# A hybrid mLSTM and sparse-attention block: moving the gate rows, a compression's gelu, a bank and a piece of a query projection

## The chip, the cores and the metric

The kernel runs on one core of a Trainium2 chip, in fp32. Its engines are TensorE (PE; its weight loads are listed as PEld), VectorE (DVE), ScalarE (ACT), GpSimd (POOL) and SyncE (SP, which here only issues transfers). Each works off its own queue of instructions in order. The metric is the device time of one execution in microseconds (us), the median of several.

## The reference, cut to what matters

One transformer block on 512 tokens of width 1024: a projection of the normed input feeds an mLSTM with 4 heads and an attention with 8 heads in 2 groups; then come the output projection, a feed-forward layer with a convolution, and a gated embedding. Only the beginning of it is touched by the change:

```
z = rms_norm(x, ln1_g) @ w_in
mq, mk, mv, mo, mi, mf, aq, akc, avc, aks, avs, akw, avw, ag = split(z)

def mlstm(q, k, v, i_pre, f_pre):              # in chunks; per head:
    b = cumsum(log_sigmoid(f_pre))             # forget gates, summed along the tokens
    a = bL - b + i_pre
    m = maximum(b + m_before, max(D))          # D = b_t - b_s + i_s for s <= t
    ...

def compress(t, pe, w1, w2):                   # for keys (Kc) and for values (Vc)
    blk = t[:, :, cidx] + pe                   # 31 blocks of 32 tokens
    return gelu(flat @ w1) @ w2

s_c = qblk @ Kc - slope * dist                 # scores: compressed, selected and window
```

## The kernel before, in words

**Products in three parts.** A weight `w` is split into a rounded high part (`hi`, a copy on ACT, L151) and the rest (`lo`, a subtraction on DVE, L152), and so is the input (`xh`, `xl`). A product is `hi*xh + hi*xl` for all its blocks, then `lo*xh`. PE therefore asks for a weight's high split when a job starts and for its low split after two thirds of the job. Two buffers hold high splits and two hold low ones, so a split waits until PE has left the job two before it.

**The stream.** `Stream` holds jobs (weight, function that writes its matmuls) in the order k1 q00 m0 w00 q01 w01 m1 w10 m2 w11 m3, then q10 q11, mo0 to mo3, mq0 to mq7. q, k, mo and mq are 8 blocks of 512 columns into a bank of tag G; m0 to m3 (`mv` in the trace) sum the mLSTM's values over two blocks each into four banks (the pair of tag Sa and two of tag T); wXY is half Y of the first compression product of kv = X (0 keys, 1 values; `cw` in the trace), 16 small blocks each. When a job starts, the split of the next one is written. Each piece of matmuls adds its planned length to the stream's clock `now`, and `after(us, fn)` lets a function write its instructions when `now` has come so far. `until(name)` writes jobs until one is done; `fill(us)` writes so much work of the stream between other things.

**What is written between the jobs.** `mlstm_gates` transposes the gate columns gz to rows (PE, `pgt`, a bank of tag V) and computes gf, gi, gt on 4 partitions (DVE L650 to L652, ACT Exp and Ln L653, L654). `mlstm_sums` does two scans and three elementwise operations on DVE (L659 to L665), an Exp (L666) and the maxima gmr (L668, L669); `mlstm_gate_columns` transposes the results back (PE L676, `pgc`, tag G). `cmp_gelu` reads a compression's sum `pc` (copy hc, L514) and does gelu with a Tanh (L515 to L520); `cmp_turn` transposes it (`pct`, L525); `cmp_second` multiplies by w2 and writes the compressed keys into K or the values into Vc. `mv_done` copies the four mv sums out of their banks into vo (ACT, L583). Then the scores begin: `scores` (L754 to L779) for group 0's last 128 tokens writes s_3a (the bank pair Sa) and s_3b (the bank Sb), with `fill` behind each of the four heads; value products, further scores and the rest of the stream follow, then the mLSTM, the output projection and the later layers.

**Banks.** Sa is one pair, Sb and V one bank each, G and T two each. A tile of a tag waits until the tile that had its bank is read out. `pc` of both kv is in Sb here.

**The order.** The program's text gives priorities, and a planner puts each engine's instructions in an order by its own durations for them: an instruction that it reckons blocked is passed by later ones. `behind(a, b)` ties a after b on their engine without a wait. What the planner has settled, each engine does in that order, whatever the real durations are.

The function `split`, and the end of the preparation as it is before:

```python
    st.after(T_GATES, mlstm_gates)       # T_GATES = 22.0, T_GC = 14.0
    st.until("cw11")
    mlstm_sums()
    st.until("mv3")
    mixa = main.tile([128, 2, 4, S], F32R, tag="mixa", name="mixa")
    mv_done()
    st.after(T_GC, mlstm_gate_columns)
```

Of the kernel before, what the change touches and what calls it, by code (L numbers as in the profile page):

```python
# [11 lines left out]
AF = mybir.ActivationFunctionType  # L12
ALU = mybir.AluOpType
# [12 lines left out]
W1 = WT + 3 * 128  # L26
KO = 4
NWARM = 9
T_GC = 14.0
T_XC = (2.0, 13.0)  # L30
T_GATES = 22.0
T_CT = 8
T_CS = 3.0
CPOS = (1, 2, 2, 2)
NSC = (0, 2)
# [28 lines left out]
def f32(ap):  # L64
    return ap.bitcast(F32)
# [3 lines left out]
def hybrid_block_kernel(ctx: ExitStack, tc: tile.TileContext, a, out):  # L69
    nc = tc.nc  # L70
    TE, VE, SE, GE = nc.tensor, nc.vector, nc.scalar, nc.gpsimd
# [8 lines left out]
    def bank(tag, bufs, n, name):  # L80
        shape = [128, 512] if n == 1 else [128, n, 512]
        return psum.tile(shape, F32, tag=tag, bufs=bufs, name=name)
# [4 lines left out]
    def pSb(name):  # L87
        return bank("Sb", 1, 1, name)

    def pG(name):  # L90
        return bank("G", 2, 1, name)
# [4 lines left out]
    def pV(name):  # L96
        return bank("V", 1, 1, name)
# [7 lines left out]
    def t2k(name, dt=F32):  # L105
        return tmp.tile([128, 512], dt, tag="t2k", name=name)
# [41 lines left out]
    def split(name, raw, shape):  # L148
        hi = wpool.tile(shape, F32R, tag="hi", name=name + "h")
        lo = wpool.tile(shape, F32R, tag="lo", name=name + "l")  # L150
        SE.activation(hi, raw, AF.Copy)  # L151
        lows[name] = VE.tensor_sub(lo, raw, f32(hi))  # L152
        if name == "q00":
            behind(lows[name], stats_done["n1"], "the norm comes first")
        return hi, lo

    lows = {}
    early = [None]

    def behind(later, sooner, why, wait=False):  # L160
        kind = mybir.DependencyClass.Sync if wait else mybir.DependencyClass.NoSync
        tc.add_manual_dep(later.ins, sooner.ins.name, mybir.DependencyInfo(kind, mybir.DependencyReason.DATA),
                          reason=why)
# [75 lines left out]
    st = Stream()  # L239
# [51 lines left out]
    def rstd_stats(acc, name, n=S, eps=EPS):  # L291
        ch = [(t0, min(128, n - t0)) for t0 in range(0, n, 128)]
        nt = len(ch)
        ps = pV(name + "ps")
        for i, (t0, w) in enumerate(ch):
            TE.matmul(ps[0:w, i:i + 1], acc[:, t0:t0 + w], ones1, start=True, stop=True)
        v = small.tile([128, 4], F32, tag="nrv", name=name + "v")
        if n % 128:
            VE.memset(v, 1.0)
        full = n // 128  # L300
        if full:
            VE.tensor_scalar(v[:, 0:full], ps[:, 0:full], 1.0 / D, eps, op0=ALU.mult, op1=ALU.add)
        if n % 128:
            w = n % 128
            VE.tensor_scalar(v[0:w, full:nt], ps[0:w, full:nt], 1.0 / D, eps, op0=ALU.mult, op1=ALU.add)
        y = newton_rsqrt(v[:, 0:nt], nt, name)
        yc = small.tile([128, 4], F32, tag=name + "yc", bufs=1, name=name + "yc")
        stats_done[name] = VE.tensor_copy(yc[:, 0:nt], y)
        return yc
# [91 lines left out]
    rc1 = rstd_stats(acc1, "n1")  # L401
# [67 lines left out]
    cx = {}  # L469
# [23 lines left out]
    def cmp_job(kv, c):  # L493
        def run(wh, wl):
            if c == 0:
                cx[kv] += (pSb(f"pc{kv}"),)
            Xh, Xl, pc = cx[kv]
            for j in range(8):
                jj = 8 * c + j
                TE.matmul(pc[0:62, 0:128], Xh[:, jj], wh[:, j], start=(jj == 0), stop=False)  # L500
                TE.matmul(pc[0:62, 0:128], Xl[:, jj], wh[:, j], start=False, stop=False)
                yield 0.11
            for j in range(8):
                jj = 8 * c + j
                TE.matmul(pc[0:62, 0:128], Xh[:, jj], wl[:, j], start=False, stop=(jj == 15))
                yield 0.06
            if c == 1:
                cmp_gelu(kv, pc)
        st.add(f"cw{kv}{c}", a["cmp_w1"][:, kv, c], [128, 8, 128], run)

    def cmp_gelu(kv, pc):
        hc = t2k(f"hc{kv}")
        h0, h1, h2 = hc[0:62, 0:128], hc[0:62, 128:256], hc[0:62, 256:384]
        SE.activation(h0, pc[0:62, 0:128], AF.Copy)  # L514
        VE.tensor_mul(h1, h0, h0)  # L515
        VE.tensor_scalar(h1, h1, GELU_A, 1.0, op0=ALU.mult, op1=ALU.add)
        VE.tensor_mul(h1, h1, h0)
        SE.activation(h1, h1, AF.Tanh, scale=GELU_C)
        VE.tensor_scalar(h1, h1, 0.5, 0.5, op0=ALU.mult, op1=ALU.add)
        VE.tensor_mul(h2, h1, h0)  # L520
        st.after(T_CT, lambda: cmp_turn(kv, h2))

    def cmp_turn(kv, h2):
        pt = (pG if kv else pV)(f"pct{kv}")
        TE.transpose(pt[:, 0:62], h2, ident[0:62, 0:62])  # L525
        gt = t2k(f"gt{kv}")
        VE.tensor_copy(gt[:, 0:62], pt[:, 0:62])
        st.after(T_CS, lambda: cmp_second(kv, gt))

    def cmp_second(kv, gt):  # L530
        p2 = (pG if kv else pV)(f"pc2{kv}")
        if kv == 0:
            TE.matmul(p2[:, 0:62], w2[:, 0], gt[:, 0:62], start=True, stop=True)
            for g in range(2):
                SE.activation(K[:, g, 0, 0:31], p2[:, g * 31:(g + 1) * 31], AF.Copy)
                VE.tensor_sub(K[0:64, g, 1, 0:31], p2[0:64, g * 31:(g + 1) * 31], f32(K[0:64, g, 0, 0:31]))
        else:
            for g in range(2):
                TE.matmul(p2[0:31, g * 64:(g + 1) * 64], gt[:, g * 31:(g + 1) * 31], w2[:, 1, 0:64],
                          start=True, stop=True)  # L540
                SE.activation(Vc[0:31, g, 0:64], p2[0:31, g * 64:(g + 1) * 64], AF.Copy)
                VE.tensor_sub(Vc[0:31, g, 64:128], p2[0:31, g * 64:(g + 1) * 64], f32(Vc[0:31, g, 0:64]))
                VE.tensor_copy(Vc[32:63, g], f32(Vc[0:31, g]))
# [33 lines left out]
    def mv_done():  # L577
        nonlocal vo
        vo = main.tile([128, NT * VW + 4 * S], F32, tag="B16", bufs=3, name="vo")
        for i in range(NT):  # L580
            vi = vo[:, i * VW:(i + 1) * VW].rearrange("p (h d) -> p h d", h=4)
            GE.memset(vi[:, :, 128:130], 1.0)
            SE.activation(vi[:, :, 0:128], psM[i].rearrange("p (h d) -> p h d", h=4),  # L583
                          AF.Copy, scale=rc1[:, i:i + 1])

    def th(h):
        return vo[:, NT * VW + h * S:NT * VW + (h + 1) * S]
# [15 lines left out]
                VE.tensor_mul(qk[:, h], ps, rb1)  # L603
        return evac

    psM = []

    def mv_job(c):
        st.add(f"mv{c}", a["w_mv"][:, 2 * c:2 * c + 2], [128, 2, 512], tokens_job(psM, 2 * c, 512))
# [31 lines left out]
    gmr = tmp.tile([128, S], F32R, tag="acc", bufs=1, name="gmr")  # L641
    gcol = consts.tile([128, 2, NT, 4], F32, name="gcol")
    grow = {}

    def mlstm_gates():
        gi_, gf_, gt_ = (t2k(nm)[0:4] for nm in ("gi", "gf", "gt"))
        pt = pV("pgt")
        for i in range(NT):
            TE.transpose(pt[0:36, i * 128:(i + 1) * 128], gz[:, i], ident)
        VE.tensor_scalar(gf_, pt[32:36], gbias[:, 1:2], None, op0=ALU.add)  # L650
        VE.tensor_scalar(gi_, pt[0:4], gbias[:, 0:1], None, op0=ALU.add)
        VE.scalar_tensor_tensor(gt_, gf_, -1.0, gf_, op0=ALU.mult, op1=ALU.min)  # L652
        SE.activation(gt_, gt_, AF.Exp)  # L653
        SE.activation(gt_, gt_, AF.Ln, bias=1.0)  # L654
        grow["r"] = gi_, gf_, gt_

    def mlstm_sums():
        gi_, gf_, gt_ = grow["r"]
        i = VE.scalar_tensor_tensor(gf_, gf_, 0.0, gt_, op0=ALU.min, op1=ALU.subtract)  # L659
        behind(i, lows["mv3"], "the weights come first")  # L660
        zero = zeroc[0:4, 0:1].to_broadcast([4, S])
        VE.tensor_tensor_scan(gt_, gf_, zero, 0.0, op0=ALU.add, op1=ALU.add)
        VE.tensor_sub(gi_, gi_, gt_)
        VE.tensor_tensor_scan(gf_, gi_, zero, 0.0, op0=ALU.max, op1=ALU.max)
        VE.tensor_add(gt_, gt_, gf_)  # L665
        SE.activation(gt_, gt_, AF.Exp, scale=-1.0)  # L666
        GE.memset(f32(gmr), 0.0)
        VE.tensor_scalar(gmr[0:4], gf_, -1.0, None, op0=ALU.mult)  # L668
        VE.scalar_tensor_tensor(gmr[32:36], gf_, -1.0, f32(gmr[0:4]), op0=ALU.mult, op1=ALU.subtract)  # L669
        grow["g"], grow["e"] = gi_, gt_  # L670

    def mlstm_gate_columns():
        pt = pG("pgc")
# [36 lines left out]
    for t, fn in zip(T_XC, blocks):  # L710
        st.after(t, fn)
    st.after(T_GATES, mlstm_gates)
    st.until("cw11")
    mlstm_sums()
    st.until("mv3")
    mixa = main.tile([128, 2, 4, S], F32R, tag="mixa", name="mixa")
    mv_done()
    st.after(T_GC, mlstm_gate_columns)

    Ec = {}  # L720

# [108 lines left out]
    groups = [(0, i) for i in (3, 2, 1, 0)] + [(1, i) for i in (0, 1, 2, 3)]  # L830
    score_cost = (0.41, 0.6, 0.82, 1.03)
    Es = []
    for r in range(4):
        Es.append(scores(*groups[0], r))
        st.spend(score_cost[3])
        st.fill(FILL2)
# [411 lines left out]
    for c in range(4):  # L1248
        st.until(f"g{c}")
        raw = wpool.tile([128, 2, 512], F32, tag="raw", bufs=2, name=f"wgr{c}")  # L1250
# [119 lines left out]
```

## Time and profile before

| | |
|---|---|
| median of the timed runs | 642.66 us (642.65 to 643.21, 3 runs) |
| the profiled execution | 640.94 us, its span 639.0 us |
| PE busy | 619.5 us, 97% of the span |
| DVE, ACT, POOL busy | 426.2, 314.2, 35.6 us |
| mean granted TensorE clock | 0.995 of full |

The span runs from the first instruction to the last; 1.9 us of the execution lie around it. All times below are counted from the span's start. A row of a timeline gives start, length, engine, line, operation, what it writes and reads, and in brackets how long the engine stood idle before it and for whom.

### The profile page before, as it was taken

What the parts mean: (1) busy time and instruction counts of PE and PEld (TensorE: products, weight loads), DVE (VectorE), ACT (ScalarE), POOL (GpSimd) and SP (SyncE); (2) the same over time, 40 slices, a digit from 0 to 9 for tenths busy, and PEclk for the clock granted to TensorE, in tenths of its full rate; (3) what the DMA queues carried; (4) which work ended last, traced back from release to release, by engine and by line L of the source; (5) the groups of instructions that cost most, each with busy time, mean ns of one, the idle gap of its engine ahead of it and who ended that gap; (6) DMA issues with size and microseconds to landing.
All of it is one profiled execution on the core that took longest, in us unless ns stands there. A gap on an engine that the chain in (4) does not pass through costs nothing. (4 is left out here: it accounts for less than half of the span.)

```text
span 639.0 us, 8426 instructions
## 1 busy us (share of the span) xinstructions
PE 619.5 (97%) x3009; PEld 499.3 (78%) x3009; DVE 426.2 (67%) x877; ACT 314.2 (49%) x657; POOL 35.6 (6%) x85
## 2 busy tenths in 40 slices
PE   9999879999999999999999999999999999999994
PEld 6888657777777776777878888888888888888884
DVE  6986677888877977785686556565656443435476
ACT  7454735677657756555545433333333323233254
POOL 0400003211111100000000000000000000000000
PEclk9999989999999999999999999999999999999998
DMA  8811133311211152112233332222222332444603
GB/s 309 301 56 67 33 99 93 106 34 33 67 54 46 34 198 87 46 34 91 74 99 99 98 99 99 97 89 92 92 97 95 98 99 98 132 133 127 203 1 132
DMA packets 23065, 63.03 MB, mean 99 GB/s; under 512 B 2728, under 2 KB 7464, under 8 KB 22956
## 3 DMA queue, kind: packets, MB, share of 16 engines
q1 hardware_dynamic: 21488, 59.93, 28.4%
q0 software_dynamic: 1248, 2.16, 1.5%
q8 instruction: 24, 0.39, 0.3%
q10 hardware_dynamic: 288, 0.41, 0.2%
q14 instruction: 17, 0.14, 0.1%
HBM read 56.72 MB, written 2.10 MB: 92 GB/s over the span
## 5 line engine op out<-in xcount | busy, mean ns | idle before, releaser
L1104 ACT ACTIVATE u<-zv 128x512 fp32r<-128x512 f32 x16 | 10.1, 634 | 45.3 <-DVE zv L1102 45.3
L1101 DVE TENSOR_TENSOR zv<-pu,n2rb 128x512 f32<-128x512 f32 x16 | 11.1, 691 | 31.3 <-PE pu L427 31.3
L807 ACT ACTIVATE ph<-pt 128x512 fp32r<-128x512 f32 x40 | 23.5, 598 | 17.0 <-PE pt L804 16.4
L808 DVE TENSOR_TENSOR pl<-pt,ph 128x512 fp32r<-128x512 f32 x40 | 27.0, 685 | 6.7 <-ACT ph L807 6.3
L777 POOL TENSOR_SCALAR E<-E,rr 128x512 f32<-128x512 f32 (+3 forms) x32 | 20.2, 631 | 158.1 <-DVE rr L774 106.5
L1091 DVE TENSOR_TENSOR zg<-pu,n2rb 128x512 f32<-128x512 f32 x16 | 11.1, 692 | 26.0 <-PE pu L427 24.5
L804 PE MATMUL pt<-cols,E 128*128 128x128 f32 x160 | 27.7, 274 | 0.4 <-DVE E L779 0.3
L804 PEld LDWEIGHTS pt<-cols,E 128*128 128x128 f32 x160 | 20.0, 140 | 6.9 <-DVE E L779 2.4
L1131 DVE TENSOR_TENSOR X<-pd,X 128x512 f32<-128x512 f32 x8 | 5.5, 692 | 29.3 <-PE pd L427 29.3
L1094 ACT ACTIVATE cv<-zg,cols 128x512 f32<-128x512 f32 x16 | 13.1, 817 | 20.1 <-DVE zg L1091 20.1
L1097 ACT ACTIVATE cv<-cv 128x512 f32<-128x512 f32 x16 | 10.1, 631 | 24.6 <-DVE cv L1096 24.6
L771 ACT ACTIVATE E<-s,nm 128x384 f32<-128x384 f32 (+2 forms) x48 | 22.2, 471 | 0.0
L812 PE MATMUL pv<-ph,V 128*128 128x512 f32 x40 | 18.7, 468 | 0.6 <-ACT ph L807 0.6
L1105 DVE TENSOR_TENSOR u<-zv,u 128x512 fp32r<-128x512 f32 x16 | 11.1, 692 | 10.5 <-ACT u L1104 10.5
L814 PE MATMUL pv<-pl,V 128*128 128x512 f32 x40 | 16.7, 418 | 0.0
L761 DVE TENSOR_REDUCE nm<-s 128x2 f32<-128x768 f32 (+2 forms) x24 | 16.4, 681 | 0.0
L1090 POOL MEMSET zg<- 128x2 f32 x16 | 1.5, 99 | 244.6 <-DVE cv L1096 151.2
L267 DVE TENSOR_TENSOR acc<-acc,sq 128x512 f32<-128x512 f32 x21 | 14.4, 685 | 0.1
L779 DVE TENSOR_SCALAR E<-E,rr 128x512 f32<-128x512 f32 (+3 forms) x32 | 13.1, 411 | 0.1
L988 PEld LDWEIGHTS mo<-vo,mw 128*128 128x128 f32 x80 | 11.4, 191 | 2.1 <-issue 0.7
L771 ACT ACTIVATE Ec<-s,nm 128x32 f32<-128x32 f32 x24 | 6.8, 285 | 12.2 <-DVE nm L761 12.1
L1096 DVE SCALAR_TENSOR_TENSOR cv<-zg,cols,cv 128x512 f32<-128x512 f32 x16 | 12.0, 751 | 0.5
(1095 smaller groups left out, 2013.7 us busy)
## 6 DMA issues: line engine op xcount, KB each, us to landing
X<-in_xg SPq DMA_DIRECT2D x1, 2048.0 KB, 8.4
xo<-xturn SPq DMA_DIRECT2D x32, 64.0 KB, 2.0
wgr<-in_w_pg SPq DMA_DIRECT2D x4, 512.0 KB, 4.0
s1r<-in_w_s SPq DMA_DIRECT2D x3, 676.0 KB, 9.1
xT<-in_xg SPq DMA_DIRECT2D x3, 514.0 KB, 8.4
rawx<-in_w_mv SPq DMA_DIRECT2D x3, 512.0 KB, 7.1
Q<-hlq POOLq DMA_DIRECT2D x12, 128.0 KB, 2.8
out_y<-xo SPq DMA_DIRECT2D x3, 512.0 KB, 2.6
```

What stands on the lines that cost most here:

```text
L267: return VE.tensor_add(acc[:, :n], acc[:, :n], sq[:, :n])
L761: VE.tensor_reduce(out=nm[:, 1:3], in_=sw, axis=AX.X, op=ALU.max, negate=True)
L771: SE.activation(e, p, AF.Exp, bias=nm[:, b:b + 1], accum_out=rs[:, b:b + 1])
L777: GE.tensor_scalar(e, e, rr[:, b:b + 1], 0.0, op0=ALU.mult, op1=ALU.add)
L779: VE.tensor_scalar(e, e, rr[:, b:b + 1], None, op0=ALU.mult)
L804: TE.transpose(pt[:, r * 128:(r + 1) * 128], Es[r][:, c0:c0 + 128], ident)
L807: SE.activation(ph, pt, AF.Copy)
L808: VE.tensor_sub(pl, pt, f32(ph))
L812: TE.matmul(pv, vs, ph, start=first, stop=False)
L814: TE.matmul(pv, vs, pl, start=False, stop=last)
L1094: SE.activation(cv, zg[:, 2:S + 2], AF.Identity, scale=cw(2), bias=cols[:, C_CB + f:C_CB + f + 1])
L1096: VE.scalar_tensor_tensor(cv, zg[:, 0:S], cw(0), cv, op0=ALU.mult, op1=ALU.add)
```

## The change

Seven planned times change or are new, two ties are set anew, one is dropped, and three tiles change their bank.

- The gate rows are written at `now` = 14 instead of 22. Their sums, before written all at once behind cw11 and tied behind mv3's low split, now come 6 after the gates; the Exp and the maxima become a function of their own 10 after that, tied behind mv2's high split and cw10's low split; the gate columns follow 5 later (before: 14 behind mv3).
- The sum of the second compression (`pc1`) goes to bank V instead of Sb, the transposes and second products of the first to G instead of V.
- The first compression's gelu is written 7 after its job instead of at once, its hc copy tied behind mv2's high split; its transpose follows 4 later instead of 8. The second compression's gelu and transpose keep their times (0 and 8).
- The high split of q11 is tied behind the second vo copy.
- 1.8 us of the stream (q10) are written in front of the first score.

```diff
-T_GC = 14.0
+T_GC = 5.0
-T_GATES = 22.0
-T_CT = 8
+T_GATES = 14.0
+T_GS = 6.0
+T_CT = (4.0, 8.0)
+T_CG = 7.0
+T_GM = 10.0
+FILLV = 1.8
@@ split
-        SE.activation(hi, raw, AF.Copy)
+        highs[name] = SE.activation(hi, raw, AF.Copy)
         lows[name] = VE.tensor_sub(lo, raw, f32(hi))
+        if name == "q11":
+            behind(highs[name], vdone[1], "the scores wait for the bank")
@@ cmp_job
-                cx[kv] += (pSb(f"pc{kv}"),)
+                cx[kv] += ((pV if kv else pSb)(f"pc{kv}"),)
@@
-                cmp_gelu(kv, pc)
+                st.after(0 if kv else T_CG, lambda: cmp_gelu(kv, pc))
@@ cmp_gelu
-        SE.activation(h0, pc[0:62, 0:128], AF.Copy)
+        i = SE.activation(h0, pc[0:62, 0:128], AF.Copy)
+        if kv == 0:
+            behind(i, highs["mv2"], "the weights come first")
@@
-        st.after(T_CT, lambda: cmp_turn(kv, h2))
+        st.after(T_CT[kv], lambda: cmp_turn(kv, h2))
@@ cmp_turn, cmp_second
-        pt = (pG if kv else pV)(f"pct{kv}")
+        pt = pG(f"pct{kv}")
-        p2 = (pG if kv else pV)(f"pc2{kv}")
+        p2 = pG(f"pc2{kv}")
@@ mv_done
-            SE.activation(vi[:, :, 0:128], psM[i].rearrange("p (h d) -> p h d", h=4),
-                          AF.Copy, scale=rc1[:, i:i + 1])
+            vdone.append(SE.activation(vi[:, :, 0:128], psM[i].rearrange("p (h d) -> p h d", h=4),
+                                       AF.Copy, scale=rc1[:, i:i + 1]))
@@ mlstm_gates
         grow["r"] = gi_, gf_, gt_
+        st.after(T_GS, mlstm_sums)
@@ mlstm_sums
-        i = VE.scalar_tensor_tensor(gf_, gf_, 0.0, gt_, op0=ALU.min, op1=ALU.subtract)
-        behind(i, lows["mv3"], "the weights come first")
+        VE.scalar_tensor_tensor(gf_, gf_, 0.0, gt_, op0=ALU.min, op1=ALU.subtract)
...
         VE.tensor_add(gt_, gt_, gf_)
-        SE.activation(gt_, gt_, AF.Exp, scale=-1.0)
+        st.after(T_GM, mlstm_maxima)
+
+    def mlstm_maxima():
+        gi_, gf_, gt_ = grow["r"]
+        i = SE.activation(gt_, gt_, AF.Exp, scale=-1.0)
+        behind(i, highs["mv2"], "the weights come first")
         GE.memset(f32(gmr), 0.0)
-        VE.tensor_scalar(gmr[0:4], gf_, -1.0, None, op0=ALU.mult)
+        i = VE.tensor_scalar(gmr[0:4], gf_, -1.0, None, op0=ALU.mult)
+        behind(i, lows["cw10"], "the weights come first")
         VE.scalar_tensor_tensor(gmr[32:36], gf_, -1.0, f32(gmr[0:4]), op0=ALU.mult, op1=ALU.subtract)
         grow["g"], grow["e"] = gi_, gt_
+        st.after(T_GC, mlstm_gate_columns)
@@ the end of the preparation, and in front of the first score
-    st.until("cw11")
-    mlstm_sums()
     st.until("mv3")
-    st.after(T_GC, mlstm_gate_columns)
...
     Es = []
+    st.fill(FILLV)
     for r in range(4):
```

## Rows read from the trace of the kernel before

**Rows 1.** The page's first part: each engine's busy time, share of the span and instructions.

```profile
PE 619.5 (97%) x3009; PEld 499.3 (78%) x3009; DVE 426.2 (67%) x877; ACT 314.2 (49%) x657; POOL 35.6 (6%) x85
```

**Rows 2.** The waits of PE over the whole span, longest first: who waited for whom, us in total, times, longest.

```profile
PE s_3a L754 <- ACT vo L583: 3.2, 1, 3.2
PE pc L500 <- ACT hc L514: 2.4, 1, 2.4
...
PE pv L812 <- DVE phc L801: 1.0, 3, 0.4
...
PE pv L812 <- ACT ph L807: 0.6, 2, 0.4
```

**Rows 3.** Stretches of the span: the stretch, its length, busy time of PE, PEld, DVE, ACT and POOL (instructions), the mean granted clock, DMA share and GB/s.

```profile
67.65:70.10 2.45, 0.03 (x2) 0.03 (x1) 0.83 (x2) 2.41 (x5) 0.00 (x0) 1.00 0.00 0
70.10:84.00 13.90, 13.90 (x96) 11.60 (x97) 10.57 (x18) 5.98 (x9) 0.00 (x0) 1.00 0.23 75
86.10:89.36 3.26, 0.01 (x1) 0.00 (x0) 2.41 (x7) 2.45 (x5) 0.00 (x0) 1.00 0.50 158
89.36:93.00 3.64, 3.64 (x12) 2.94 (x13) 1.45 (x4) 2.81 (x8) 0.00 (x0) 0.55 0.47 151
...
200.00:220.00 20.00, 19.93 (x110) 15.71 (x109) 17.35 (x49) 13.55 (x42) 3.10 (x4) 1.00 0.13 44
```

**Rows 4.** The timeline of PE, from q01 to the first compression's transpose.

```profile
54.55 0.45 PE L423 MATMUL pq<-x1h,q01h 128*128 128x512 f32 x1
...
58.27 1.98 PE L427 MATMUL pq<-x1h,q01l 128*128 128x512 f32 x8
...
65.68 1.97 PE L341 MATMUL pmv<-mv1l,x1h 128*128 128x512 f32 x8
70.08 0.27 PE L500 MATMUL pc<-cw10h,cXh 128*62 128x128 f32 x1 [2.42 <-ACT hc L514]
...
73.69 0.27 PE L525 MATMUL pct<-cols,hc 62*128 62x62 f32 x1
```

**Rows 5.** The timeline of ACT over the same stretch.

```profile
58.47 1.06 ACT L151 ACTIVATE mv1h<-rawx 128x1024 fp32r<-128x1024 f32 x1 [3.13 <-PE pq L424]
63.74 0.63 ACT L653 ACTIVATE gt<-gt 4x512 f32<-4x512 f32 x1 [4.21 <-DVE gt L652]
64.39 1.28 ACT L654 ACT_TABLE_LOAD   x1
65.68 0.63 ACT L654 ACTIVATE gt<-gt 4x512 f32<-4x512 f32 x1
...
68.81 1.06 ACT L151 ACTIVATE cw10h<-rawx 128x1024 fp32r<-128x1024 f32 x1
69.77 0.25 ACT L514 ACTIVATE hc<-pc 62x128 f32<-62x128 f32 x1
```

**Rows 6.** The timeline of DVE over the same stretch, and the first and last of the row sums.

```profile
54.27 1.22 DVE L152 TENSOR_TENSOR q01l<-q01r,q01h 128x1024 fp32r<-128x1024 f32 x1 [1.42 <-ACT q01h L151]
...
60.34 1.23 DVE L152 TENSOR_TENSOR mv1l<-rawx,mv1h 128x1024 fp32r<-128x1024 f32 x1 [3.70 <-ACT mv1h L151]
61.59 0.74 DVE L650 TENSOR_SCALAR gf<-pgt,cols 4x512 f32<-4x512 f32 x1
...
63.03 0.67 DVE L652 SCALAR_TENSOR_TENSOR gt<-gf 4x512 f32<-4x512 f32 x1
63.63 0.67 DVE L553 SCALAR_TENSOR_TENSOR zq<-pq,n1rb 128x512 f32<-128x512 f32 x1
64.23 1.17 DVE L489 TENSOR_TENSOR cXl<-cX,cXh 128x992 fp32r<-128x992 f32 x1
...
79.33 0.67 DVE L659 SCALAR_TENSOR_TENSOR gf<-gf,gt 4x512 f32<-4x512 f32 x1
...
83.24 0.68 DVE L665 TENSOR_TENSOR gt<-gt,gf 4x512 f32<-4x512 f32 x1
```

**Rows 7.** The timeline of ACT and PE around the first scores.

```profile
83.06 1.98 PE L341 MATMUL pmv<-mv3l,x1h 128*128 128x512 f32 x8
...
83.95 0.64 ACT L666 ACTIVATE gt<-gt 4x512 f32<-4x512 f32 x1 [3.79 <-DVE gt L665]
...
86.91 0.31 ACT L518 ACTIVATE hc<-hc 62x128 f32<-62x128 f32 x1 [2.17 <-DVE hc L517]
...
88.07 2.38 ACT L583 ACTIVATE vo<-pmv,n1yc 128x512 f32<-128x512 f32 x4
...
89.36 0.56 PE L754 MATMUL s_3a<-K,Q 128*128 128x272 f32 x2 [3.25 <-ACT vo L583]
```

**Rows 8.** The timeline of PE: a matmul of q10 right behind the gap, and two neighbours later.

```profile
91.69 0.63 PE L424 MATMUL pq<-x1l,q10h 128*128 128x512 f32 x1
...
95.75 0.39 PE L424 MATMUL pq<-x1l,q10h 128*128 128x512 f32 x1
95.98 0.40 PE L423 MATMUL pq<-x1h,q10h 128*128 128x512 f32 x1
```

**Rows 9.** The timelines of PE and DVE: the second compression's products, the last reading of their bank, and the first use of Vc.

```profile
97.46 0.30 PE L539 MATMUL pc<-w,gt 128*31 128x64 f32 x2
...
100.42 0.21 DVE L542 TENSOR_TENSOR Vc<-pc,Vc 31x64 fp32r<-31x64 f32 x1
...
117.21 0.47 PE L812 MATMUL pv<-phc,Vc 128*128 128x512 f32 x1 [0.25 <-DVE phc L801]
```

More of the change, by code (lines that the diff above doesn't have):

```diff
@@ L155, in split @@
         return hi, lo
-    lows = {}
+    lows, highs = {}, {}
     early = [None]
@@ L604, in mq_evac @@
         return evac
-    psM = []
+    psM, vdone = [], []
     def mv_job(c):
```

## The prediction, written before the changed kernel was run

> **What bounds the kernel now.** I read the page's busy shares first: TensorE (PE) is busy for 97% of the span, VectorE (DVE) for 67%, ScalarE (ACT) for 49% [rows 1]. So the end is set by PE, and only PE's idle time and the time it spends at a lower clock can be won. The table of PE's waits comes next: two single waits, 3.2 us of the scores (s_3a) on the vo copies and 2.4 us of the second compression (pc) on a copy of hc, stand far above the rest, and both lie in the part of the kernel that the diff touches [rows 2]. The table of stretches puts them at 67.65 and 86.1 us and shows a third loss: after the second gap the granted clock is 0.55 on average for 3.64 us, after the first it stays 1.00 [rows 3]. The timelines then say why each gap is there.
>
> First gap. PE ends mv1 at 67.65 and starts cw10 at 70.08 [rows 4]. cw10 needs its high split and its accumulation bank, which is the bank of the first compression, read out by the hc copy. ACT works these off in one order: it stands idle for 4.21 us until the gate row gt exists (63.74), does Exp, a table load of 1.28 us and Ln, then four Q copies, and only then, at 68.81, the split cw10h and at 69.77 the hc copy [rows 5]. The gate row is late since its three DVE operations stand behind mv1l, from 61.59 to 63.70 [rows 6].
>
> Second gap. mv3 ends on PE at 85.0. s_3a writes the bank pair in which two of the mv sums lie, so it needs the first two vo copies. On ACT these stand behind the hc copy of the second compression, its Tanh (2.17 us of waiting for DVE) and the split q11h, and start at 88.07; four take 2.38 us, PE goes on at 89.36 [rows 7]. PE has one q10 pair to do in between and then nothing. Behind the gap a q10 matmul of 512 columns takes 0.63 us, later 0.39, with 0.23 from start to start [rows 8]: this is the 1.2 GHz level against 2.4. At 0.55 of the clock 3.64 us do the work of 2.00, so the low clock costs 1.64 us.
>
> **The change, part by part.** I place the moved steps by the stream's own clock (now = 0 at the start of k1, which is 36.8 us in the trace; a 512-column job is 5.16, a compression half 1.36).
>
> (a) Bank of cw10 and cw11: V instead of Sb; the transposes and second products of kv = 0 go from V to G. cw10 no longer waits for the hc copy of the first compression, and the first score no longer for the second's. V's earlier tenant, the gate transposes, is read by two DVE operations, which end long before 67.65 once they move as in (b). So one of the two things that end the first gap is taken away; the other is cw10h.
>
> (b) Gate rows. The transposes move from now = 22 to 14, into the low part of mv0 (trace: 51.7 instead of 60.08). They are PE work of the same length: 0. Their three DVE operations (0.74 + 0.74 + 0.67 = 2.15 us) then stand behind the Q subtractions that end at 52.85, where DVE is idle until 54.27: 1.42 us hidden, and q01l and cw01l slide by 0.7, with PE asking for q01l at 58.27 and getting it at 56.2. Exp, load and Ln (0.63 + 1.28 + 0.63 = 2.54) need gt at 55.0; ACT is idle from 55.33 to 58.47, 3.13 us [rows 5, 6]. So they fit and ACT is free from 59.53, where cw10h can go as soon as a buffer is free (cw01 ends its high half at 61.5) instead of at 68.81. Cost 0, and the first gap goes: -2.42.
>
> (c) The five row sums (0.67 + 1.21 + 0.68 + 1.21 + 0.68, with their gaps 4.58 us from 79.33 to 83.91) move to now = 20.3, about 58.3. DVE is idle from 56.64 to 60.34, so 2 us are hidden at once; the rest pushes cXl, zq and mv1l (1.17 + 0.67 + 1.23) from 62.9 to about 66.0. PE asks for mv1l at 65.68: I take 0.2. Bounds: 0 if mv1l goes first, 1.4 if the two Q subtractions (0.69 each) go ahead of it too.
>
> (d) The first compression's gelu is written 7 after its job and its hc copy tied behind mv2h, which waits until PE leaves mv1's high half (65.68) and, on ACT, for the four Q copies. With (c) zq is done at about 64.4, the Q copies at 67.0, mv2h at 68.1; PE asks for mv2h at 69.2. Behind it come the last Exp (0.64), hc at about 69, cw11h, Tanh; from the hc copy to the transpose pct the trace has 3.92 us (69.77 to 73.69) [rows 4, 5], which gives 73 to 74, and the planned place of pct (now = 34.8, late in mv2's low part) is about 74.5. The compressed keys are asked for by s_3a at 83 only, and their last products are planned at now = 37.8, 78.4 us. Cost 0; the cover is mv2, 5.7 us of matmuls, and if ACT is a microsecond later PE waits as long at mv2 or pct. The maxima (0.41 + 0.68 on DVE) have the same cover. The gate columns' eight transposes move from 106.7 to the time of cw11: PE work of the same length, 0.
>
> (e) The second compression's gelu stays where it was in the text, behind cw11. Before, the last Exp stood in front of it on ACT and waited for the sums until 83.95 [rows 7]; with the Exp gone the hc copy can follow cw11 (now about 77) and its chain of 3.9 us ends by 81.5, before mv3 does (83: 2.42 earlier than 85.0 and 0.6 later for the gate columns). So ACT is free when the mv sums are ready, and q11h is tied behind the second vo copy. Two copies are 2.38 / 2 = 1.2 us; meanwhile PE has s_3b and the piece of q10 (1.8 asked for, five pairs: 2.15 planned, 5 x 0.455 = 2.3 us by the 0.23 spacing). -3.25, and with the gap the low clock goes: -1.64. q11h is asked for only behind the rest of q10 and two heads' scores. The q10 work is brought forward, not added: 0. Without this cover (one pair, 0.5 us) PE would wait about 0.7.
>
> (f) With the q10 piece in front, q10 ends about 0.9 us of matmuls behind the second head's scores, where the second compression's last products also hold a bank of G: from 97.46 to 100.63 in the trace, 3.2 us [rows 9]. q11 then needs q10's bank, whose reading (zq, 0.69) stands on DVE behind the maxima of those scores (0.19 + 0.69 + 0.68). In the trace the scores lay between q10 and q11 and hid this. PE idles from about 1.2 to 2.7 us behind the scores, 1.5; bounds 0 (planned around, with other matmuls first) and 2.5 (DVE one split, 1.2, later, less what PE finds). I take 1.0, nearer to the full wait. The values' product Vc is first used by PE at 117.21 and its bank is read out at 100.63: 16 us of slack, 0.
>
> Loads from memory: the same transfers in the same order on SP's queue; none of them ends a wait of PE [rows 2].
>
> Sum: -2.42 - 3.25 - 1.64 = -7.31; +0.2 +1.0 = -6.1. The profiled execution took 640.94, 1.7 below the median of the timed runs, 642.66; the sum is taken from both alike: 634.8 and 636.55. I say **636.5 us** in the timed runs. The likeliest case's own range is 634 to 639: from 642.66 - 7.31 = 635.35 with a microsecond for small waits of the score stage that may go too, up to both upper bounds, 635.35 + 1.4 + 2.5 = 639.2.
>
> **Rivals.**
>
> *A gap stays, whole or in part* (the change doesn't do what it says). The order on each engine is a planner's, by its own durations; it put one q10 pair in front of s_3a and was 3.25 us wrong. If vo is late again, only the first gap goes: 642.66 - 2.42 = 640.2. If instead mv2h or cw10l is late, ACT being dense from 64.4 to 74, part of the first gap comes back 1.5 us further on: 638. Against the first: what stood in front of vo is tied or done by 81.5. Chances 0.10 and 0.04.
>
> *The score stage starts worse*: (f) at its upper bound and one more such wait where three users of G meet, 635.35 + 0.2 + 3.2 = 638.8. For it: the transpose pct of the second compression and its products meet q10 and q11 in two banks; against it: the planner lets later matmuls pass a blocked one (s_3b and the q10 pair stand in front of s_3a). Chance 0.10.
>
> *The gate rows hold up ACT.* If the planner puts Exp in front of q01h, ACT stands until 55.0, Ln ends at 57.5, q01h at 58.6, and PE, which needs it at 54.5, idles 4.1 us and pays 1.64 for the clock: 642.66 - 7.31 + 5.7 = 641.1; with the other small costs 642. That ACT holds everything behind a late instruction is what rows 5 and 7 show at 63.74 and 86.91. The Trainium skill says it as a rule (PSUM — Partial Sum Buffer, Engine vs sequencer instructions): ScalarE's, VectorE's and GpSimd's queues are strict FIFO. By that rule each tie of this diff is a risk, since a copy tied behind mv2h or vo stops all later ones too; the trace agrees that the queue stops (4.21 and 2.17 us), and by my times nothing behind the ties is due. Chance 0.10: 0.06 no change, 0.04 slower.
>
> *Slower: DVE becomes the bound of the score stage.* From 200 to 220 DVE is busy 17.35 of 20 us, PE 19.93 [rows 3]; the 2.15 us of stream work that are spent in front of the first score are missing as filler later, and the whole stage is ordered anew. 48 value units follow; if each waits 0.2 us for its copies, that is 9.6: 642.66 - 7.31 + 9.6 = 645. It decides from (7.31 + 1.3) / 48 = 0.18 us a unit. For it: the busy share; against it: the waits of pv on phc and ph are 1.6 us in all now [rows 2], 0.03 a unit, and work of the stream is left when the stage ends (72.2 planned, 63 asked for by the fills before, 64.8 then). Chance 0.11: 0.08 slower, 0.03 no change.
>
> *Forecast:* the remaining 0.55.
>
> **Chances.** A change of under 0.2% (1.3 us) can't be told from none here. Faster: 0.55 + 0.10 + 0.04 + 0.10 = 0.79. Same: 0.06 + 0.03 = 0.09. Slower: 0.04 + 0.08 = 0.12. The range for 8 in 10 takes in the forecast, the first two rivals and the middle of the third: 633.8 to 641.3.
>
> **What would show it.** Right: no PE wait above 1.5 us between 40 and 110; clock 1.00 there; gt's Exp and Ln near 55 to 58; cw10h before 66; the second hc copy near 77; vo starting within 0.5 us of mv3's end, near 83. Wrong: a PE gap at 54.5 (Exp before q01h), at 65.7 (mv1l, above 0.5 us), at mv2 (mv2h), at 74 (pct), at the start of s_3a; a clock under 1.00 behind any of them; or an end that moved less than the start of the scores did, by more than the 1.0 of (f).

## The result, and the profile after

| | before | after |
|---|---|---|
| median of the timed runs, same chip | 642.85 us (642.65 to 643.21, 4 runs) | 635.55 us (634.64 to 635.95, 4 runs) |
| ratio to before | | 0.9891, 95% interval 0.9879 to 0.9904 |
| the profiled execution, its span | 640.94, 639.0 us | 634.64, 632.8 us |
| mean granted clock | 0.995 | 0.996 |

The kernel became 7.3 us faster by the medians (1.1%; their own ratio, 0.9886, lies inside the interval). 636.5 was predicted, with 633.8 to 641.3 as the range. On other chips before took 642.18, 641.96 and 641.72 us, so the experiments below are compared by their ratio to the runs of before on their own chip.

The waits of PE in the kernel after, longest first, in the columns of [rows 2]:

```profile
PE pv L824 <- DVE phc L813: 1.5, 5, 0.4
...
PE poa L429 <- ACT mixa L839: 1.1, 1, 1.1
PE s L766 <- ACT E L783: 0.2, 1, 0.2
```

Both large waits of [rows 2] are gone. New is 1.1 us of poa on mixa, where the output projection starts. Before, the same table had:

```profile
PE poa L423 <- ACT mixa L827: 0.2, 1, 0.2
```

The stretches of after that answer to [rows 3], in the same columns:

```profile
51.80:84.00 32.20, 32.14 (x217) 26.66 (x216) 24.49 (x39) 18.40 (x27) 0.00 (x0) 1.00 0.27 77
84.00:86.20 2.20, 2.20 (x11) 1.82 (x10) 0.00 (x0) 2.20 (x5) 0.00 (x0) 1.00 0.22 89
...
200.00:220.00 20.00, 20.00 (x112) 15.30 (x110) 18.19 (x50) 15.52 (x49) 4.08 (x5) 1.00 0.11 30
```

PE stands still for 0.06 us between 51.8 and 84, and the clock is 1.00 in all three. From 200 to 220, in the score stage, DVE is busier than in [rows 3] (18.19 of 20 us against 17.35) and PE is busy all the time.

The timeline of ACT in after, which answers to [rows 5] and the ACT rows of [rows 7]:

```profile
53.72 1.06 ACT L155 ACTIVATE q01h<-q01r 128x1024 fp32r<-128x1024 f32 x1
55.56 0.63 ACT L661 ACTIVATE gt<-gt 4x512 f32<-4x512 f32 x1 [0.78 <-DVE gt L660]
...
57.51 0.63 ACT L662 ACTIVATE gt<-gt 4x512 f32<-4x512 f32 x1
...
64.50 0.64 ACT L564 ACTIVATE Q<-zq 64x512 fp32r<-64x512 f32 x1 [3.97 <-DVE zq L561]
...
67.11 1.06 ACT L155 ACTIVATE cw10h<-rawx 128x1024 fp32r<-128x1024 f32 x1
68.08 1.04 ACT L155 ACTIVATE mv2h<-rawx 128x1024 fp32r<-128x1024 f32 x1
...
79.25 1.06 ACT L155 ACTIVATE q10h<-q10r 128x1024 fp32r<-128x1024 f32 x1 [3.88 <-DMA q10r<-in_w_in]
80.22 0.25 ACT L520 ACTIVATE hc<-pc 62x128 f32<-62x128 f32 x1
...
83.69 2.42 ACT L591 ACTIVATE vo<-pmv,n1yc 128x512 f32<-128x512 f32 x4 [0.93 <-PE pmv L347]
```

Exp, load and Ln lie at 55.56 to 58.14, in a hole that ACT had before. cw10h starts at 67.11 where it started at 68.81 [rows 5], the vo copies at 83.69 instead of 88.07 [rows 7], and ACT now waits for PE with them, not PE for ACT. The timelines of DVE and PE, which answer to [rows 4], [rows 6], the PE rows of [rows 7], [rows 8] and [rows 9]:

```profile
53.42 0.74 DVE L658 TENSOR_SCALAR gf<-pgt,cols 4x512 f32<-4x512 f32 x1
...
58.17 0.68 DVE L668 SCALAR_TENSOR_TENSOR gf<-gf,gt 4x512 f32<-4x512 f32 x1 [1.51 <-ACT gt L662]
...
63.19 0.68 DVE L673 TENSOR_TENSOR gt<-gt,gf 4x512 f32<-4x512 f32 x1
...
64.39 1.20 DVE L156 TENSOR_TENSOR mv1l<-rawx,mv1h 128x1024 fp32r<-128x1024 f32 x1
```

```profile
66.32 1.98 PE L347 MATMUL pmv<-mv1l,x1h 128*128 128x512 f32 x8
68.23 0.27 PE L506 MATMUL pc<-cw10h,cXh 128*62 128x128 f32 x1
...
84.17 0.39 PE L430 MATMUL pq<-x1l,q10h 128*128 128x512 f32 x1
...
86.21 0.42 PE L766 MATMUL s_3a<-K,Q 128*128 128x272 f32 x2
...
90.53 0.30 PE L547 MATMUL pc<-w,gt 128*31 128x64 f32 x2
90.76 0.73 PE L433 MATMUL pq<-x1h,q10l 128*128 128x512 f32 x2
...
92.66 0.47 PE L429 MATMUL pq<-x1h,q11h 128*128 128x512 f32 x1
...
112.10 0.47 PE L824 MATMUL pv<-phc,Vc 128*128 128x512 f32 x1 [0.18 <-DVE phc L813]
240.26 0.73 PE L429 MATMUL poa<-mixa,woa0h 128*128 128x512 f32 x2 [1.11 <-ACT mixa L839]
```

The row sums, with the low split of cw01 between them, fill DVE from 58.17 to 63.87 and mv1l still ends at 65.59, before PE asks for it at 66.32. The first score starts at 86.21 behind five q10 pairs, without a wait and at full clock (0.39 us for the q10 matmul, where [rows 8] has 0.63). Vc is read at 112.10 with 0.18 us of waiting, as little as in [rows 9]. Only the last row has a wait worth naming.

Where the time went is best seen between three points: PE's first matmul of k1, its first of poa, and the end of the span. Each start is from the timeline of PE of that kernel.

```
                     k1      first poa   end      k1 to poa   poa to end
before               36.77   243.58      639.0    206.81      395.42
after                37.30   236.94      632.8    199.64      395.86
after, second time   36.28   236.28      632.5    200.00      396.22
without the piece    36.91   237.06      632.2    200.15      395.14
piece paid back      36.85   236.44      631.6    199.59      395.16
no piece, no tie     36.62   236.45      631.6    199.83      395.15
```

From k1 to poa after is 7.17 us shorter than before; the two gaps and the low clock were 2.42 + 3.25 + 1.64 = 7.31. From poa on it is 0.44 longer, with a wait that is 0.9 longer (1.1 against 0.2). In the second execution of after it is 6.81 shorter, so the agreement to 0.1 us is partly chance. The start-up in front of k1, which the change doesn't touch, took 0.53 us longer in this execution; in the rows of the table it varies by 1.0.

### The profile page after: what moved, and what is told of

Its sections match the earlier page's. It is cut to its first block, busy times and chain, and to the rows that moved or that the text cites. A ratio compares the mean times of both kernels' runs of the same rounds, so it can differ in the third digit from the quotient of the medians.

```text
span 632.8 us, 8428 instructions
## 1 busy us (share of the span) xinstructions
PE 619.7 (98%) x3009; PEld 498.9 (79%) x3009; DVE 428.1 (68%) x877; ACT 314.4 (50%) x657; POOL 35.3 (6%) x85
## 5 line engine op out<-in xcount | busy, mean ns | idle before, releaser
L992 PE MATMUL ms<-qk 128*128 128x512 f32 (+3 forms) x32 | 12.0, 458 | 0.0
```

Of the source, the lines that this page charges most:

```text
L992: TE.matmul(ps[:, j % 2, 0:n], qk[:, 4 + h, j * 128:(j + 1) * 128], qk[:, h, j * 128:S], start=True, stop=True)
```

## The experiments

In a name, "undone" or "no" means the changed kernel without that part, "alone" the kernel before with that part only. Ratios are to before on the same chip.

**The banks alone.** The bank of pc1 and those of pct0 and pc20.

```diff
-                cx[kv] += (pSb(f"pc{kv}"),)
+                cx[kv] += ((pV if kv else pSb)(f"pc{kv}"),)
...
-        pt = (pG if kv else pV)(f"pct{kv}")
+        pt = pG(f"pct{kv}")
...
-        p2 = (pG if kv else pV)(f"pc2{kv}")
+        p2 = pG(f"pc2{kv}")
```

> Kernel before with the three bank changes alone. Theory: cw10 still waits for cw10h, which ends at 69.87 against 70.02 for the hc copy: minus 0.15, no change that can be told, 642.7. Rival (the bank is half of the first gap): 641.6 or less.

Measured: 641.68 us, 0.9995 (0.9984 to 1.0006). The first compression's gap, in the timeline of PE:

```profile
69.80 0.27 PE L500 MATMUL pc<-cw10h,cXh 128*62 128x128 f32 x1 [2.27 <-ACT cw10h L151]
```

The gap is as long as before to 0.15 us and now ends with cw10h instead of the hc copy. The bank by itself is worth nothing that can be told: it takes away the last of two waits and the other ends 0.15 us earlier.

**The gate rows alone.** The planned times of gates, sums, maxima and columns, with the two ties of the maxima.

```diff
-T_GC = 14.0
-T_GATES = 22.0
+T_GC = 5.0
+T_GATES = 14.0
+T_GS = 6.0
+T_GM = 10.0
...
+        st.after(T_GS, mlstm_sums)
...
+        st.after(T_GM, mlstm_maxima)
...
-    st.until("cw11")
-    mlstm_sums()
...
```

> Kernel before with the gate rows spread alone (14 / 6 / 10 / 5 and the two ties); banks, gelu, q11 and the piece as before. Theory (the gate rows on ScalarE cause both gaps): the first gap goes wholly, since the hc copy follows cw10h in time even in the shared bank (-2.4); in the second the last Exp no longer stands in front of hc and vo (-3.25 to -2.5, a wait of up to 0.7 for two vo copies stays) and the low clock goes (-1.6): 636 to 637. Rival (the bank and the piece are needed too): only part of one gap goes, 639 to 641.

Measured: 637.36 us, 0.9922 (0.991 to 0.9933): this part carries 5.0 us of the change (4.8 by the medians). The second gap is gone. The first has moved on by one job; timelines of PE and ACT:

```profile
72.19 0.51 PE L338 MATMUL pmv<-mv2h,x1h 128*128 128x512 f32 x1 [2.28 <-ACT mv2h L153]
```

```profile
67.80 0.25 ACT L516 ACTIVATE hc<-pc 62x128 f32<-62x128 f32 x1
68.07 1.28 ACT L520 ACT_TABLE_LOAD   x1
70.88 0.31 ACT L520 ACTIVATE hc<-hc 62x128 f32<-62x128 f32 x1 [1.53 <-DVE hc L519]
71.09 1.04 ACT L153 ACTIVATE mv2h<-rawx 128x1024 fp32r<-128x1024 f32 x1
```

The first gap was expected to go wholly, and the time is above the expected 636 to 637: cw10 is in time now, but mv2h stands behind the gelu's hc copy, table load and Tanh, and the Tanh waits 1.53 us for DVE.

**The gate rows undone.** The reverse of the diff above, on the changed kernel.

```diff
-T_GATES = 14.0
+T_GATES = 22.0
...
+    st.until("cw11")
+    mlstm_sums()
...
```

> Changed kernel with the gate rows as before (22, sums behind cw11, columns 14 behind mv3). Theory: cw10h is late again (68.8), first gap 2.2; in the second the last Exp waits for the sums until 84 and Tanh behind it for VectorE, vo starts near 87, the piece covers 2.3 of it: gap near 2, no low clock. 635.6 + 2.2 + 2 = 639.8. Rival (banks, tie and piece do it alone): below 637.5.

Measured: 638.55 us, 0.9949 (0.9937 to 0.9962). Timeline of PE:

```profile
70.09 0.27 PE L506 MATMUL pc<-cw10h,cXh 128*62 128x128 f32 x1 [2.26 <-ACT cw10h L155]
...
88.60 0.36 PE L762 MATMUL s_3a<-K,Q 128*128 128x272 f32 x1 [1.16 <-issue]
```

The first gap is back at 2.26 us: gt comes late again and holds cw10h. The second is back with 1.16 of its 3.25 us, where 2 had been expected. With the piece alone (below) 2.10 are left, and there q11h (1.04 us) still runs in front of the vo copies, here behind them. So, by these two traces, the piece takes away 1.15 and the tie most of the other 0.94.

**The bank undone.**

```diff
-                cx[kv] += ((pV if kv else pSb)(f"pc{kv}"),)
+                cx[kv] += (pSb(f"pc{kv}"),)
...
-        pt = pG(f"pct{kv}")
+        pt = (pG if kv else pV)(f"pct{kv}")
...
```

> Changed kernel with the banks of before (pc1 in Sb, pct0 and pc20 in V). Theory: the hc copy of the first compression, now tied behind mv2h and behind the last Exp (71.0 in the trace), is what cw10 waits for again, PE idles from 68.2 to 71.2: plus 3.0, 638.6, or plus 4.5 with a low clock behind it. Rival (the planner lets mv2 pass cw10, the bank is worth nothing): 635.6.

Measured: 638.39 us, 0.9939 (0.9926 to 0.9952). Timeline of PE:

```profile
68.45 0.50 PE L342 MATMUL pmv<-mv2h,x1h 128*128 128x512 f32 x1 [0.88 <-ACT mv2h L155]
...
70.55 0.27 PE L506 MATMUL pc<-cw10h,cXh 128*62 128x128 f32 x1 [1.60 <-ACT hc L520]
```

The planner knows that cw10's bank is not free, sends mv2 ahead, and PE waits for mv2h and then for the hc copy, which is now behind mv2h on ACT: 2.48 us in all, as long as the first gap was. The time is near the 638.6 of the theory, but by another path: mv2 did pass cw10, as the rival had it, and the wait came all the same. So the bank is worth nothing alone and 2.4 to 3.1 us (0.9939 against 0.9891 and 0.9902) once the hc copy is delayed.

**The gelu at once.** The changed kernel with the first compression's gelu as before.

```diff
-T_CT = (4.0, 8.0)
+T_CT = (8.0, 8.0)
...
-                st.after(0 if kv else T_CG, lambda: cmp_gelu(kv, pc))
+                cmp_gelu(kv, pc)
...
-        if kv == 0:
-            behind(i, highs["mv2"], "the weights come first")
```

> Changed kernel with the first compression's gelu at once behind its job, untied, its transpose 8 later. ScalarE has hc and Tanh in front of mv2h; Tanh waits about 2 us for VectorE, mv2h ends near 71.5 instead of 69.1, and PE asks for it at 70.0: a wait of 1.5, 637.1. Rival (mv2h has room, or VectorE is quick): 635.6.

Measured: 638.45 us, 0.9945 (0.993 to 0.9961). Timeline of PE, and stretches behind the wait in the columns of [rows 3]:

```profile
71.65 0.50 PE L342 MATMUL pmv<-mv2h,x1h 128*128 128x512 f32 x1 [2.28 <-ACT mv2h L155]
```

```profile
72.00:73.00 1.00, 1.00 (x6) 0.83 (x5) 0.86 (x1) 1.00 (x2) 0.00 (x0) 1.00 0.00 0
73.00:74.00 1.00, 1.00 (x4) 0.43 (x2) 0.89 (x1) 0.07 (x1) 0.00 (x0) 0.53 0.00 0
74.00:75.00 1.00, 1.00 (x3) 0.68 (x3) 0.55 (x2) 0.00 (x0) 0.00 (x0) 0.50 0.00 0
75.00:76.00 1.00, 1.00 (x4) 0.74 (x3) 0.00 (x0) 0.00 (x0) 0.00 (x0) 0.50 0.66 152
76.00:77.00 1.00, 1.00 (x5) 0.82 (x4) 0.00 (x0) 0.00 (x0) 0.00 (x0) 0.76 0.92 356
```

A wait of 1.5 was expected. It is the same wait as with the gate rows alone, so delaying the gelu is what removes it. ACT's queue stopped behind an instruction that waits: the Tanh stood 1.52 us for DVE here, and mv2h, which needed nothing from it, with it. The Trainium skill states that as strict FIFO queues (PSUM — Partial Sum Buffer, Engine vs sequencer instructions); the trace agrees, with this 1.52 us. And here the clock fell, 1.4 us after PE had gone on: by the rows 0.47 + 0.50 + 0.50 + 0.24 = 1.7 us of work lost, the same as behind the second gap of before (1.64).

**The piece alone.** The kernel before with 1.8 us of q10 in front of the first score.

```diff
     Es = []
+    st.fill(1.8)
     for r in range(4):
```

> Kernel before with 1.8 us of the stream in front of the first score and nothing else. Theory: PE idles 3.25 - 1.8 = 1.4 instead of 3.25 in the second gap and keeps its clock: 642.8 - 1.8 - 1.6 = 639.4. Rival (the low clock comes anyway, or the piece is missed later): 641 to 643.

Measured: 641.00 us, 0.9987 (0.9971 to 1.0003), no difference that can be told. Timeline of PE, and stretches behind both gaps:

```profile
70.17 0.27 PE L500 MATMUL pc<-cw10h,cXh 128*62 128x128 f32 x1 [2.42 <-ACT hc L514]
...
90.92 0.42 PE L754 MATMUL s_3a<-K,Q 128*128 128x272 f32 x1 [2.10 <-issue]
```

```profile
70.00:74.00 4.00, 3.83 (x28) 3.54 (x29) 3.80 (x8) 3.61 (x5) 0.00 (x0) 0.58 0.00 0
...
92.00:96.00 4.00, 4.00 (x15) 2.91 (x15) 1.80 (x6) 2.07 (x7) 0.00 (x0) 0.69 0.39 130
```

The second gap shrinks from 3.25 to 2.10 only (1.4 was expected), and s_3b, which PE did in front of the gap before, now comes behind it. The clock still falls behind it, and poa waits 1.1 us for mixa: most of what the piece wins, it gives back at the end of the stage. The first gap is that of before to the hundredth (2.42), yet here the clock is 0.58 behind it, where before's profile has 1.00 [rows 3].

**No piece.** The changed kernel without it.

```diff
     Es = []
-    st.fill(FILLV)
     for r in range(4):
```

> Changed kernel without the 1.8 us of q10 in front of the first score. Theory: PE has s_3b and one q10 pair (1.0 us) while two vo copies take 1.2 us behind mv3 and start about 0.3 before its end: a wait of 0.2 to 0.7, 636.0 (plus 0.2 to 0.7). Rival (the piece carries the second gap): plus 2 or more, 637.6.

Measured: 633.91 us, 0.988 (0.9867 to 0.9894). A loss of 0.2 to 0.7 was expected, and none came: the ratio is below that of the changed kernel (0.9891), though the intervals overlap. The comparison on one chip follows below. Timelines of ACT and PE at the first score:

```profile
83.29 2.42 ACT L591 ACTIVATE vo<-pmv,n1yc 128x512 f32<-128x512 f32 x4 [1.02 <-PE pmv L347]
```

```profile
83.54 0.40 PE L766 MATMUL s_3b<-K,Q 128*128 128x512 f32 x1
...
84.05 0.48 PE L429 MATMUL pq<-x1h,q10h 128*128 128x512 f32 x1
...
84.61 0.52 PE L766 MATMUL s_3a<-K,Q 128*128 128x272 f32 x2
```

Two of the four vo copies take 1.2 us and start 0.25 us before PE leaves mv3; s_3b and the one q10 pair take 84.61 - 83.54 = 1.07. That is enough, and PE doesn't wait. And poa waits only 0.2 us for mixa, as before the change.

**No tie of q11.**

```diff
-        if name == "q11":
-            behind(highs[name], vdone[1], "the scores wait for the bank")
```

> Changed kernel without the tie of q11h behind the second vo copy. The planner puts q11h in front of vo. Its buffer comes free when PE leaves mv3's high half (82.1), it runs 82.7 to 83.7, when vo starts anyway: 0 to plus 0.3. Theory: 635.7. Rival (the tie is needed): the vo copies start a microsecond later and PE waits, 636.6 or more.

Measured: 635.46 us, 0.9906 (0.9894 to 0.9919), no gap at the scores. The tie is worth nothing that can be measured while the gate rows are early.

**Four on one chip,** to tell what the piece costs and why. The changed kernel again:

> The changed kernel once more, beside the next three on one chip. Every theory: 0.989 of the time before, the wait of 1.1 us for mixa at the end of the score stage.

Measured: 634.90 us (634.30 to 635.53), 0.9902 (0.9885 to 0.9918). Without the piece again:

> The changed kernel without the piece of q10 in front of the scores. Theory A (the piece takes 1.8 us of matmuls away from the score stage, where they are missing as filler at the end): no wait of more than 0.3 us for mixa, 0.8 to 1.5 us faster than the changed kernel of the same chip. Theory B (the earlier lead of the kernel without the piece was drift between chips): within 0.3 us of it.

Measured: 634.17 us (633.96 to 634.50), 0.9888 (0.9873 to 0.9902), 0.73 below it, where theory A wanted 0.8 to 1.5. The intervals overlap, so by time alone theory B isn't refuted. The trace speaks against it: the wait for mixa is 0.2 again, and the stretch from poa to the end is 1.08 shorter (395.14 against 396.22). With the piece, and as much less fill behind the fourth head's scores:

```diff
-        st.fill(FILL2)
+        st.fill(FILL2 - (FILLV if r == 3 else 0.0))
```

> The changed kernel with the piece, but the fill in front of the fourth head's scores made 1.8 us smaller, so that the same amount of stream work is left for the rest of the score stage as without the piece. Theory A: the wait for mixa falls from 1.1 to below 0.3 us, and the time is within 0.5 us of the kernel without the piece. Theory C (the piece costs by its place, since q10 then ends earlier and q11's bank or the order of the first heads gets worse): the time stays with the changed kernel, 0.8 us or more above the one without the piece, whatever the wait for mixa does.

Measured: 633.40 us (633.09 to 633.50), 0.9874 (0.986 to 0.9889), the lowest median of all (its runs overlap those of the last one below), and 1.5 below the changed kernel with no overlap of the runs. Theory C is out: with the piece in the same place and the amount paid back, the time doesn't stay. The first poa matmuls that need the last mixa, in the timelines of PE of the changed kernel (second time) and of this one:

```profile
239.60 0.73 PE L429 MATMUL poa<-mixa,woa0h 128*128 128x512 f32 x2 [1.11 <-ACT mixa L839]
```

```profile
238.65 0.73 PE L429 MATMUL poa<-mixa,woa0h 128*128 128x512 f32 x2 [0.19 <-ACT mixa L839]
```

The wait falls by 0.92, and the stretch from poa to the end is 1.06 shorter (396.22 to 395.16), as in both kernels without the piece. In the tables of waits every kernel with the piece has this wait at 1.1 (after in both executions, the piece alone, no tie, and the gate rows, the bank and the gelu undone), and every kernel without it, or with it paid back, has it at 0.2. So theory A holds for that part. It missed the size: the kernel should have come within 0.5 us of the one without the piece and is 0.77 faster. By the three points these 0.6 us of span lie between k1 and poa (199.59 against 200.15). The stretches place them between 100 and 150 us, without the piece and with it paid back, in the columns of [rows 3]:

```profile
100.00:150.00 50.00, 48.52 (x262) 37.74 (x262) 41.94 (x109) 34.60 (x106) 10.34 (x18) 1.00 0.23 64
```

```profile
100.00:150.00 50.00, 49.35 (x264) 37.51 (x264) 42.89 (x112) 34.83 (x109) 10.51 (x18) 1.00 0.25 66
```

PE idles 1.48 us there without the piece (by the waits: pv 0.6 for phc, s and pt 0.5 and 0.3 for E) and 0.65 with it paid back. Three traces of the changed kernel without the piece have 1.46 to 1.50 there; after in both executions and this one have 0.45 to 0.65. So the piece, written early, also takes about 0.9 us of waiting out of this part of the score stage; why it does, no run shows. The last one, without piece and tie:

> The changed kernel without the piece and without the tie of q11's split behind the second vo copy. If the tie alone keeps the vo copies in time once the piece is gone, q11h goes ahead of them and the first scores wait 0.3 to 1.2 us, with 0.3 to 1.2 us in the time. If the early gate rows alone keep them in time, no wait there and the time of the kernel without the piece.

Measured: 633.56 us (633.25 to 633.99), 0.9878 (0.9863 to 0.9893). Here the planner puts q11h in front of the vo copies; timelines of ACT and PE:

```profile
81.80 1.05 ACT L155 ACTIVATE q11h<-q11r 128x1024 fp32r<-128x1024 f32 x1
83.00 2.42 ACT L589 ACTIVATE vo<-pmv,n1yc 128x512 f32<-128x512 f32 x4
```

```profile
84.32 0.40 PE L764 MATMUL s_3a<-K,Q 128*128 128x272 f32 x1
```

It does no harm: ACT was idle then, and the copies start where mv3's sums let them. So neither the piece nor the tie is needed to keep the copies in time; with the gate rows alone the second gap was gone too.

## Why the prediction was right, and where it was not

**The two gaps and the clock behind the second** (2.42 + 3.25 + 1.64 = 7.31). Right in place and size: 7.17 us came out between k1 and poa (6.81 in the second execution). The cause was named right too: the late gate rows, at both gaps a wait of ACT for gt, in front of everything else on ACT. Moving the gate rows alone gives 5.0 us and undoing them loses 3.0 to 3.7 (0.9949 against 0.9891 and 0.9902).

**(a) and (d), the bank and the gelu.** That the bank takes away one of two waits was right, and alone it did nothing. What (d) said only in passing, that PE waits as long at mv2 if ACT is late, is the heart of it: without the delay the gelu stands in front of mv2h and 2.28 us come back. The times inside were too hopeful. cw10h was to start before 66; the planner put the four Q copies in front and it starts at 67.11, ends at 68.17, and PE uses it at 68.23: 0.06 us to spare, where (b) had it free to go from 61.5. The second hc copy was to come near 77 and came at 80.22, since q10h stands in front of it and waits for its weight until 79.25; I had not looked for that transfer among ACT's waits. The table load of 1.28 us that ACT did in front of the Tanh before (at 70.99) now comes in front of the last Exp (at 69.14), which (d) didn't count, so the first hc copy came at 70.97 and not near 69. None of the three made PE wait.

**(c) +0.2 and (f) +1.0.** Neither appeared. mv1l was done 0.73 us before it was asked for, as the planner let it pass the two Q subtractions and cXl. For (f), the planner ran q10's low part in front of the second head's scores, with the second compression's products between (90.53), and q11 starts behind those scores at 92.66 without a wait. I had weighed this, as the lower bound of (f), and took the value nearer the full wait. In their place came the 0.44 from poa on, with its wait of 0.9, and the 0.53 of the start-up, which has nothing to do with the change: 7.17 - 0.44 - 0.53 = 6.2. So the sum on the trace was nearly right by exchange and by luck: 640.94 - 6.1 = 634.8 was said of the profiled execution, 634.64 was measured.

**(e), the piece as a cover.** Wrong. "Without this cover PE would wait about 0.7" counted both copies from the end of mv3, though they start 0.25 us earlier, and half a microsecond of matmuls where s_3b and the pair are 1.07; without the piece PE waits for nothing. "The q10 work is brought forward, not added: 0" is where the cost lay: work of the stream that is spent early is missing later. My last rival had the sentence ("missing as filler later"), but with DVE as its mechanism and the value units as its place. The units lost nothing in sum: pv's waits for phc and ph are 1.5 us now and were 1.6 [rows 2]. Within the stage, PE idles about 0.9 us less between 100 and 150 with the piece than without it, and 0.4 to 0.5 more between 150 and 200 (1.42 and 1.33 in both traces of after, 0.93 to 0.95 in three of the changed kernel without the piece). The main place of the loss is the end of the stage, where poa needs the last mixa and nothing is left to put in between; paying the 1.8 us back behind the fourth head's scores takes the 0.9 away.

**From the profile to the median.** I took the same sum from the profiled execution, 640.94, and from the median, 642.66, as if the 1.7 us between them had nothing to do with the change. That gave 636.5, 0.95 too high. In 41 timed executions of before on three chips the mean granted clock and the time go together: 7 with 0.993 to 0.995 took 640.24 to 641.19 us, 34 with 0.988 to 0.992 took 641.22 to 643.25, medians 640.45 and 642.1. By an estimate from [rows 3], 3.64 us at 0.55 lower the mean by 3.64 x 0.45 / 639 = 0.003. The profile of before is of the first kind, with the clock at 1.00 behind the first gap; the piece alone, with the same gap, shows 0.58 behind it. So most executions of before seem to have lost some 1.6 us there as well, which went with the gap and wasn't in my sum. That is inferred: no trace of before itself shows its first gap with the clock down. The kernel with the bank undone, where only this gap is left, splits in the same way: two executions at 0.998 took 636.71 and 637.07 us, four at 0.993 to 0.995 took 638.25 to 639.08.

**The other rivals.** No gap stayed. Exp was not put in front of q01h (it starts at 55.56, after a wait of 0.78, behind q01h). Both were fair risks: with the gate rows, the bank or the gelu undone, 2.3 to 2.5 us of waiting are back each time, at mv2 or cw10.

## What to carry to other kernels

When two long waits hang on late instructions at the head of an in-order queue, move what produces them, and then read what comes to stand in front of the next wanted instruction: here the gate rows only moved the first gap on (2.42 to 2.28 us) until the gelu was delayed, and the bank was worth nothing until then. When filler is written earlier, ask which later fill can spare as much, and take it out there in the same edit; here the end of the stage paid otherwise. Before a sum is taken from a median, look whether the profiled execution is like the others (its time and its granted clock), since the profile may lack a loss that most executions have.

## What the runs showed of the hardware that was not expected

A stand of PE of 2.3 to 2.4 us was followed by a low clock in some executions and not in others. The clock stayed at 1.00 behind 2.42 us in before [rows 3] and behind 2.26 to 2.28 with the gate rows alone, the bank alone and the gate rows undone; it fell to 0.50 behind 2.42 us with the piece alone, and behind 2.28 us with the gelu at once, there 1.4 us after PE had gone on. It also fell behind the 2.10 us of the piece alone. Behind the 2.42 and 2.28 us it cost 1.7 us of work (with the piece alone, 4 us at 0.58). One profile can thus price a gap of this length wrongly.
